# Mixture-of-experts stage: gathered tokens in batches of four chunks, half of the transposes in another PSUM bank, one bias sum

## The chip, the core and the metric

One core of a Trainium2 chip runs the kernel as one program. The time is device time in microseconds (us) of one execution. Runs of the kernel before lie at 1731.54, 1734.95 and 1739.19 us, median 1734.95 us. The profile is one execution of its own.

## The reference, cut to what matters

The program is two transformer layers over 256 tokens of width 1024. Only the last part matters here: 32 experts, each token goes to 4 of them. The experts' weights are 32 x (1024 x 2048 + 1024 x 1024) float32 numbers.

```python
logits = xt @ w_router + b_router
top_val, top_idx = lax.top_k(logits, TOP_K)          # 4 of 32
gates = softmax(top_val)
# for each expert e, with the rows xb of its tokens:
hb = clamped_swiglu(xb @ w_gu[e] + b_gu[e])          # 1024 -> 2 x 1024
yb = hb @ w_down[e] + b_down[e]                      # 1024 -> 1024
y[tok] += gate * yb
```

## The kernel before, in words

Everything up to the router takes the first 740 us and is not touched. Then comes the loop over experts (`for e in range(NE - 2)`, L1635), which is what the change edits. Each expert gets 64 token places (`CAP`).

**Weights.** A weight tile is 128 partitions x 16 KB, 2 MB in all. An expert has four such tiles of `w_gu` and two of `w_down`. They land in a ring of twelve slots (`slot_tile`, L1469): the tile of number n may be loaded when the last reader of tile n - 12 is through. All loads are issued by SyncE's queue (SP) in one order, that of the program: the four tiles of gate and up of expert e+1, then the two of down of expert e. The bias matrix `b_down` takes a slot of this ring too: `load_b_down` (L1401) is called in iteration 15, after the tiles of that iteration, and its slot goes on to the twelfth tile behind it, which is the second down tile of expert 17.

**One iteration e.** `make(0)` and `make(1)` (L1524) turn the two halves of the gate and up result of expert e with four TensorE transposes each into a PSUM bank, from where VectorE and ScalarE make the activation `u_`. `front(e + 1)` runs the gate and up product of the next expert (L1511, 64 instructions, 8 in each of 8 steps k). Inside it, after given k, stand `make(1)`, the `scatter` of expert e-1 (L1566, adds the expert's output to the four accumulator banks) and `slots_of(e)` (L1444 and L1445, tokens to places). Last comes `dn_product` (L1556, 32 instructions), whose bank is read by ScalarE into `yh` (L213) and by VectorE into `yl` (L214).

**Gathering tokens.** Every second iteration (e even) `group` makes the inputs of the next two experts. `chunk(c)` (L1456) is four TensorE instructions for 128 of the 1024 features, 128 columns wide, into a bank with the tag `tr`, and one evacuation into `xg` by VectorE (L1462). Eight chunks stand between the steps of `dn_product`. `xg` has one buffer, so that its first chunk can be written only when the product that reads the old one has ended.

**PSUM.** Eight banks: four accumulators, two with the tag `mm` for the gate and up product, one `tr`, one `y`. `tr` serves the transposes of `make(0)` and `make(1)`, `turn_slots`, the chunks and the transposes of the gates; `y` serves the down product.

**Bias of the down product.** `add_b_down(odd)` (L1405) runs after the down products of iterations 15 and 16, each time with its own copy and transposes of the gates and with four products (eight instructions) over half of the columns. It is the last reader of the bias slot.

**Order.** The program's order is a first draft. The framework plans the order of each engine's instructions from its own table of costs, keeps the order within a queue fixed from then on, and sets the semaphores; the trace shows the order that came out. Each engine works its queue in order. After the loop follow a branch for experts with more than 64 tokens (L1606), the last two experts and the final norm.

Of the kernel before, what the change touches and what calls it, by code (L numbers as in the profile page):

```python
# [11 lines left out]
F32 = mybir.dt.float32  # L12
# [5 lines left out]
ALU = mybir.AluOpType  # L18
# [4 lines left out]
P = 128  # L23
T = 256
# [3 lines left out]
NE = 32  # L28
# [15 lines left out]
def kernel(ctx: ExitStack, tc: tile.TileContext, A, out, probe=None, stop=None):  # L44
# [46 lines left out]
    def ps(name, tag="mm"):  # L91
        return pst["pool"].tile([P, 512], F32, tag=tag, name=name, bufs=pst["tags"][tag])
# [177 lines left out]
    def half(h):  # L270
        return slice(h * 512, (h + 1) * 512)
# [1120 lines left out]
        V.tensor_copy(cnt_i[:, NE:NE + 1], cmax)  # L1392

    yh, yl, sT = (mp.tile([P, w], F32R, name=t) for t, w in (("yh", 512), ("yl", 512), ("sT", T)))
    u_ = mp.tile([P, 2, 4, CAP], F32, name="u_")
    bd = {}

    def load_b_down():  # L1400
        bd["t"] = slot_tile()  # L1401
        for q in range(4):
            ld(bd["t"][q * NE:(q + 1) * NE, :256], A["b_down_2"][0, :, q * 256:(q + 1) * 256])

    def add_b_down(odd):  # L1405

        g4 = small.tile([P, 2, 4, NE], F32, tag="SX", name="g4", bufs=1)
        V.tensor_copy(g4, gate.unsqueeze(2).to_broadcast([P, 2, 4, NE]))
        bd4, gT = bd["t"][:, :256], bd["t"][:, 256:512]
        pt = ps("gT_ps", "tr")  # L1410
        for b in range(2):
            PE.transpose(pt[:, b * P:(b + 1) * P], g4[:, b].rearrange("p q e -> p (q e)"), ident)
        V.tensor_copy(gT, pt[:, :T])
        for b in range(2):
            for h in range(2):
                q = 2 * h + odd
                rows_ = slice(q * NE, (q + 1) * NE)
                PE.matmul(acc[b][h][:, odd * 256:(odd + 1) * 256], gT[rows_, b * P:(b + 1) * P], bd4[rows_, :],
                          start=False, stop=False, tile_position=(q * NE, 0))

    def one_hot(pos_cols, n, name):

# [7 lines left out]
    def norm_hot(pos_cols, n, name):  # L1430

        s_ = small.tile([P, 2, n, CAP], F32, tag="SX", name=f"SX{name}", bufs=1)
        for b in range(2):
            for o in range(n):
                last["V"] = V.tensor_scalar(s_[:, b, o, :], iota_s, pos_cols[:, b, o:o + 1], rm[:, b:b + 1],
                                            op0=ALU.is_equal, op1=ALU.mult)
        return s_
# [13 lines left out]
    def gather(s_, n, name, xg=None):  # L1451

        if xg is None:
            xg = small.tile([P, 8, n * CAP], F32, tag="xg", name=f"xg{name}", bufs=1)

        def chunk(c, on_v=False, tag="tr"):  # L1456
            po = ps(f"xg{name}_{c}", tag)
            for b in range(2):
                PE.matmul(po[:, :n * CAP], x_t[:, b, every(2, c)], s_[:, b].rearrange("p o s -> p (o s)"),  # L1459
                          start=b == 0, stop=b == 1)  # L1460
            if on_v:
                V.tensor_scalar(xg[:, c, :], po[:, :n * CAP], ffn_g(c), None, op0=ALU.mult)  # L1462
            else:
                S.activation(xg[:, c, :], po[:, :n * CAP], AF.Copy, scale=ffn_g(c))
        return xg, chunk

    slot = [len(gu0)]

# [52 lines left out]

    def swiglu(gs, bcol, name, u_=u_):

        def make(h):  # L1524
            pt = ps(f"gt{name}_{h}", "tr")
            for c in range(4):

                PE.transpose(pt[:, c * P:(c + 1) * P], gs[:, every(4, 4 * h + c)], ident)  # L1528
            pv = pt.rearrange("p (c q s) -> p c q s", c=4, q=2)

            g_, t_ = (gs[:, 512 * h + 256 * i:512 * h + 256 * (i + 1)].rearrange("p (c s) -> p c s", c=4)
                      for i in range(2))
            u = u_[:, h]
            V.tensor_tensor(g_, pv[:, :, 0, :],  # L1534
                            bcol[:, 4 * h:4 * h + 4].unsqueeze(2).to_broadcast([P, 4, CAP]), op=ALU.add)
            V.tensor_tensor(u, pv[:, :, 1, :],  # L1536
                            bcol[:, 8 + 4 * h:12 + 4 * h].unsqueeze(2).to_broadcast([P, 4, CAP]), op=ALU.add)
            V.tensor_scalar(g_, g_, 7.0, None, op0=ALU.min)  # L1538
            V.tensor_scalar(u, u, 7.0, -7.0, op0=ALU.min, op1=ALU.max)
            S.activation(t_, g_, AF.Tanh, scale=0.851)  # L1540
            V.scalar_tensor_tensor(u, u, 1.0, g_, op0=ALU.add, op1=ALU.mult)
            V.scalar_tensor_tensor(u, t_, 1.0, u, op0=ALU.add, op1=ALU.mult)
        return make

    def dn_product(wt, gslot, name, chunk=None, u_=u_, tag="y", between=None):

        po = ps(f"dn{name}", tag)
        for k in range(8):
            if chunk:
                chunk(k, True)  # L1550
            for f in (between or {}).get(k, ()):
                f()
            if k % 4 == 0:
                w = wt(k // 4)
            for cg in range(2):
                PE.matmul(po[cg * CAP:(cg + 1) * CAP, :], u_[:, k // 4, k % 4, :],  # L1556
                          w[:, k % 4, cg * 512:(cg + 1) * 512], start=k == 0, stop=k == 7)
        hilo(yh, yl, po, scale=gslot() if callable(gslot) else gslot)
# [17 lines left out]

    def group(g):
        pos_cols = pos1[:, :, g * GR:(g + 1) * GR]
        st["xg"], chunk = gather(norm_hot(pos_cols, GR, f"g{g}"), GR, f"g{g}")
        return chunk  # L1580

    def front(e, between):
        if e == EOVER + 1:
# [7 lines left out]
    def slots_of(e):  # L1591
        st["gslot", e] = turn_slots(one_hot(pos1[:, :, e:e + 1], 1, f"e{e}")[:, :, 0], gate3[:, :, e, :], f"e{e}")

    chunk = group(0)
    first = {k: [lambda k=k: chunk(k + 1, k % 2 == 0, ("tr", "y")[(k + 1) % 2])] for k in range(1, 7)}
    first[0] = [lambda: chunk(0), lambda: chunk(1, True, "y")]
    first[1].append(lambda: seed(1))
# [4 lines left out]
    def overflow():  # L1602
        wsl = [slot_tile() for _ in range(2)]
        oxg = st["keep"][:, D:D + D // 2].rearrange("p (c s) -> p c s", c=8)
        most = nc.values_load(cnt_i[0:1, NE:NE + 1], min_val=0, max_val=T)
        with tc.If(most > CAP):  # L1606
            with tc.For_i(0, NE, 1) as e:
                ne = nc.values_load(cnt_i[0:1, bass.ds(e, 1)], min_val=0, max_val=T)
                with tc.If(ne > CAP):
                    pc = small.tile([P, 2, 1], F32, tag="pc", name="pc", bufs=1)  # L1610
                    gc = small.tile([P, 2, 3], BF16, tag="gc", name="gc", bufs=1)
                    bc = small.tile([P, 16], F32, tag="bc", name="bc", bufs=1)
                    V.tensor_copy(pc, pos1[:, :, bass.ds(e, 1)])
                    V.tensor_copy(gc, gate3[:, :, bass.ds(e, 1), :].rearrange("p b o q -> p b (o q)"))
                    V.tensor_copy(bc, bgu[:, :, bass.ds(e, 1)].rearrange("p c o -> p (c o)"))

                    def by_turns(src, n):
                        return lambda m: piece(src, m, wsl[m % 2], n)

                    for blk in range(1, T // CAP):  # L1620
                        V.tensor_scalar(pc, pc, float(CAP), None, op0=ALU.subtract)
                        _, chunk = gather(norm_hot(pc, 1, f"o{blk}"), 1, f"o{blk}", oxg)
                        s_ = one_hot(pc, 1, f"o{blk}")
                        gslot = turn_slots(s_[:, :, 0], gc, f"o{blk}")
                        wg = w_gu[bass.ds(e, 1)].rearrange("o k c -> (o k) c")
                        wd = w_dn2[bass.ds(e, 1)].rearrange("o k c -> (o k) c")
                        g0 = gu_out(gu_product(by_turns(wg, 2), oxg, 0, f"o{blk}",
                                               {k: [lambda k=k: chunk(k)] for k in range(8)}), f"o{blk}")
                        make = swiglu(g0, bc, f"o{blk}")
                        make(0)  # L1630
                        make(1)
                        dn_product(by_turns(wd, 4), gslot, f"o{blk}")
                        scatter()

    for e in range(NE - 2):  # L1635
        make = swiglu(gs, bgu[:, :, e], f"e{e}")
        make(0)
        between = {1: [lambda: make(1)], 4: [lambda: slots_of(e)]}
        if e and e - 1 != EOVER:
            between[3] = [scatter]  # L1640
        gs = front(e + 1, between)
        wd = load_dn(w_dn2[e])
        if e == 15:
            load_b_down()
        if e == EOVER:

            wg1 = load_gu(w_gu[e1])
            wd0, wd1 = load_dn(w_dn2[e0]), load_dn(w_dn2[e1], parts=True)
        if e == 2:
            counts()  # L1650
        chunk = group(e // GR + 1) if e % GR == 0 else None
        dn_product(wd, st["gslot", e], f"e{e}", chunk)
        if e in (15, 16):
            add_b_down(e - 15)

    scatter()
    overflow()
# [69 lines left out]
```

## Time and profile before

| | |
|---|---|
| runs | 1731.54, 1734.95, 1739.19 us (median 1734.95) |
| the profiled execution's own time | 1733.49 us |
| its span, first to last instruction | 1731.8 us |
| TensorE matmul (PE) busy | 1634.4 us, 94% |
| VectorE (DVE) busy | 744.4 us, 43% |
| ScalarE (ACT) busy | 511.2 us, 30% |
| granted TensorE clock, mean | 0.991 |
| DMA moved | 527.57 MB, mean 305 GB/s |

The share of busy time is a mean over very different stages. For the expert loop one looks at two of its iterations at a time (an even and an odd one, since only even ones gather), at what TensorE waits for in them, and at the rate at which the weights arrive. A row of a timeline gives the start and the length in us, engine, line, operation, output and inputs, the shape, how many instructions are merged in it, and in brackets how long the engine sat idle before it and which operation ended that.

### The profile page before, as it was taken

Reading aid. Unit: us, or ns where it says so; the run is one execution under the profiler, and the core shown is the slowest. Engines: PE = TensorE matmul, PEld = TensorE weight load, DVE = VectorE, ACT = ScalarE, POOL = GpSimd, SP = SyncE. Lnnn points to the kernel's source line nnn. Section 1 sums busy time; section 2 is a strip of 40 time slices with the busy share of each in tenths; the row PEclk is TensorE's granted clock in tenths of the full one; section 3 lists DMA queues with packets and bytes.
Section 4 is the critical chain, followed back from the end, with each engine's and each line's share of the span. In section 5 each row is a group of like instructions: output and inputs, shape, how many; then the busy total and the mean of one; then the engine's idle time right before and its main releaser. Section 6 shows DMA issues by size and latency. Waiting matters only on the chain. (4 is left out here: it accounts for less than half of the span.)

```text
span 1731.8 us, 23231 instructions
## 1 busy us (share of the span) xinstructions
PE 1634.4 (94%) x9279; PEld 1014.7 (59%) x9280; DVE 744.4 (43%) x1705; ACT 511.2 (30%) x959; POOL 221.5 (13%) x319
## 2 busy tenths in 40 slices
PE   8899999999999999999999999999999999999987
PEld 8887799989999788863333333333333333333332
DVE  5867755567777776533232222212222321222113
ACT  4465554555555565521110110001101100110011
POOL 6988412200010000000000000000000000000000
PEclk9999999999999999999999999999999999999999
DMA  9852355654646535489999999999949999999992
GB/s 287 255 166 67 104 183 184 217 192 161 214 147 207 162 126 192 171 354 427 428 425 428 428 427 428 428 427 427 399 177 426 428 427 427 426 428 428 426 425 106
DMA packets 139413, 527.57 MB, mean 305 GB/s; under 512 B 11105, under 2 KB 99206, under 8 KB 114694
## 3 DMA queue, kind: packets, MB, share of 16 engines
q1 hardware_dynamic: 139302, 526.05, 77.3%
q8 instruction: 74, 1.21, 0.3%
q14 instruction: 37, 0.30, 0.1%
HBM read 524.95 MB, written 4.22 MB: 306 GB/s over the span
## 5 line engine op out<-in xcount | busy, mean ns | idle before, releaser
L1511 PE MATMUL gue<-raw,xgg 128*64 128x512 f32 x2032 | 455.6, 596 | 0.0
L189 DVE TENSOR_TENSOR wl<-raw,wh 128x1024 fp32r<-128x1024 f32 (+3 forms) x218 | 273.8, 1257 | 179.0 <-ACT wh L188 178.5
L188 ACT CAST wh<-raw 128x1024 fp32r<-128x1024 f32 (+2 forms) x220 | 227.8, 1035 | 257.7 <-PE g L197 64.7
L1511 PEld LDWEIGHTS gue<-raw,xgg 128*64 128x64 f32 x2032 | 138.6, 137 | 254.9 <-issue 242.4
L1556 PE MATMUL dne<-raw,u__8494 128*64 128x512 f32 x992 | 234.0, 607 | 0.0
L1462 DVE TENSOR_SCALAR xgg<-xgg,v_c 128x128 f32<-128x128 f32 x124 | 43.5, 351 | 387.9 <-PE gue L1511 195.5
L1519 ACT COPY gse<-gue 128x512 f32<-128x512 f32 x62 | 36.3, 586 | 345.7 <-PE gue L1511 345.7
L1556 PEld LDWEIGHTS dne<-raw,u__8494 128*64 128x64 f32 x992 | 65.4, 138 | 109.9 <-issue 100.9
L1459 PEld LDWEIGHTS xgg<-SXg,x_t 128*128 128x128 f32 x512 | 70.1, 196 | 99.1 <-DVE xgg L1462 57.6
L1459 PE MATMUL xgg<-SXg,x_t 128*128 128x128 f32 x512 | 94.2, 307 | 34.0 <-DVE xgg L1462 33.0
L1687 POOL TENSOR_TENSOR ssl<-ssl,nhalf 128x1 f32<-128x1 f32 x2 | 1.1, 558 | 969.2 <-DVE ssl L1686 969.2
L1534 DVE TENSOR_TENSOR gse<-gte,bgu 128x256 f32<-128x256 f32 x62 | 26.3, 425 | 194.6 <-PE gte L1528 185.8
L213 ACT ACTIVATE yh<-dne,gslote 128x512 fp32r<-128x512 f32 x32 | 22.0, 688 | 253.5 <-PE dne L1556 253.5
L388 POOL TENSOR_TENSOR convo<-convo,prod 128x256 f32<-128x256 f32 x90 | 76.9, 854 | 7.4
L1540 ACT ACTIVATE gse<-gse 128x256 f32<-128x256 f32 x62 | 25.8, 417 | 165.5 <-DVE gse L1538 165.5
L196 PE MATMUL g<-h_h,wh 128*128 128x256 f32 x256 | 73.1, 286 | 0.0
L197 PE MATMUL g<-h_l,wh 128*128 128x256 f32 x256 | 73.1, 285 | 0.0
L198 PE MATMUL g<-h_h,wl 128*128 128x256 f32 x256 | 72.9, 285 | 0.0
L1528 PEld LDWEIGHTS gte<-ident,gse 128*128 128x128 f32 x248 | 35.7, 209 | 62.5 <-issue 49.5
L387 POOL TENSOR_SCALAR prod<-hconv,v_c 128x256 f32<-128x256 f32 x90 | 68.0, 756 | 8.6
L1536 DVE TENSOR_TENSOR u__8494<-gte,bgu 128x256 f32<-128x256 f32 x62 | 26.0, 419 | 74.7 <-PE dne L1556 74.7
L1528 PE MATMUL gte<-ident,gse 128*128 128x128 f32 x248 | 49.7, 314 | 8.7 <-DVE u__8494 L1536 8.7
(804 smaller groups left out, 3047.3 us busy)
## 6 DMA issues: line engine op xcount, KB each, us to landing
raw<-in_w_gu_dram SPq DMA_DIRECT2D x127, 2048.0 KB
raw<-in_w_down_dram SPq DMA_DIRECT2D x63, 2048.0 KB
raw<-in_w_in_dram SPq DMA_DIRECT2D x32, 1024.0 KB
raw<-in_w_up_dram SPq DMA_DIRECT2D x22, 1024.0 KB
raw<-in_w_down_dram SPq DMA_DIRECT2D x12, 1024.0 KB
raw<-in_w_out_dram SPq DMA_DIRECT2D x8, 1024.0 KB
raw<-in_w_ckv_dram SPq DMA_DIRECT2D x8, 1024.0 KB
raw<-in_w_in_dram SPq DMA_DIRECT2D x13, 512.0 KB
```

The lines of the kernel that those rows point to most:

```text
L188: S.copy(hi, src)
L189: last["lo"] = (eng or V).tensor_sub(lo, src, hi.bitcast(F32))
L196: PE.matmul(o, wh[:, k, :], ah[:, k, :], start=first and k == 0, stop=False)
L197: PE.matmul(o, wh[:, k, :], al[:, k, :], start=False, stop=False)
L198: PE.matmul(o, wl[:, k, :], ah[:, k, :], start=False, stop=last and k == nk - 1)
L387: G.tensor_scalar(prod[0][:, :T], hconv[:, c, k:k + T], w, 0.0, op0=ALU.mult, op1=ALU.add)
L388: G.tensor_add(convo[:, c, :], convo[:, c, :], prod[0][:, :T])
L1459: PE.matmul(po[:, :n * CAP], x_t[:, b, every(2, c)], s_[:, b].rearrange("p o s -> p (o s)"), start=b == 0, stop=b == 1)
L1462: V.tensor_scalar(xg[:, c, :], po[:, :n * CAP], ffn_g(c), None, op0=ALU.mult)
L1511: PE.matmul(pgu[n][cg * CAP:(cg + 1) * CAP, :], xg[:, k, col:col + CAP], w[:, k % 2, cg * D + n * 512:cg * D + (n + 1) * 512], start=k == ...
L1528: PE.transpose(pt[:, c * P:(c + 1) * P], gs[:, every(4, 4 * h + c)], ident)
L1556: PE.matmul(po[cg * CAP:(cg + 1) * CAP, :], u_[:, k // 4, k % 4, :], w[:, k % 4, cg * 512:(cg + 1) * 512], start=k == 0, stop=k == 7)
```

## The change

Three edits, all in the expert loop.

1. `gather` gets a third function, `four(h)`: it puts four chunks side by side into one `tr` bank (4 x 128 columns) and evacuates them with one VectorE operation, which multiplies with the gains spread over the columns. `four(0)` stands ahead of step 0 of the down product, `four(1)` ahead of step 4, in place of eight chunks. The first group keeps its chunks.
2. `make(1)` writes its transposes to the bank `y` in place of `tr`, in all iterations of the loop.
3. The bias sum is done once, in iteration 15: `b_down` is loaded as two halves of 512 columns (two DMAs in place of four), `gates_down` turns the gates ahead of step 4 of the down product, `add_b_down` adds four products of 512 columns ahead of step 6.

```diff
     def load_b_down():
         bd["t"] = slot_tile()
-        for q in range(4):
-            ld(bd["t"][q * NE:(q + 1) * NE, :256], A["b_down_2"][0, :, q * 256:(q + 1) * 256])
+        for h in range(2):
+            ld(bd["t"][h * NE:(h + 1) * NE, :512], A["b_down_2"][0, :, half(h)])
...
+    def gates_down():
+        g2 = small.tile([P, 2, 2, NE], F32, tag="SX", name="g2", bufs=1)
+        V.tensor_copy(g2, gate.unsqueeze(2).to_broadcast([P, 2, 2, NE]))
         pt = ps("gT_ps", "tr")
         for b in range(2):
-            PE.transpose(pt[:, b * P:(b + 1) * P], g4[:, b].rearrange("p q e -> p (q e)"), ident)
-        V.tensor_copy(gT, pt[:, :T])
+            PE.transpose(pt[:2 * NE, b * P:(b + 1) * P], g2[:, b].rearrange("p q e -> p (q e)"), ident)
+        V.tensor_copy(bd["t"][:2 * NE, 512:512 + T], pt[:2 * NE, :T])
+    def add_b_down():
         for b in range(2):
             for h in range(2):
-                q = 2 * h + odd
-                rows_ = slice(q * NE, (q + 1) * NE)
-                PE.matmul(acc[b][h][:, odd * 256:(odd + 1) * 256], gT[rows_, b * P:(b + 1) * P], bd4[rows_, :],
-                          start=False, stop=False, tile_position=(q * NE, 0))
+                rows_ = slice(h * NE, (h + 1) * NE)
+                PE.matmul(acc[b][h], bd["t"][rows_, 512 + b * P:512 + (b + 1) * P], bd["t"][rows_, :512],
+                          start=False, stop=False, tile_position=(h * NE, 0))
...
+        def four(h, tag="tr"):
+            po = ps(f"xg{name}_h{h}", tag)
+            w = n * CAP
+            for i in range(4):
+                for b in range(2):
+                    PE.matmul(po[:, i * w:(i + 1) * w], x_t[:, b, every(2, 4 * h + i)],
+                              s_[:, b].rearrange("p o s -> p (o s)"), start=b == 0, stop=b == 1)
+            gains = vec["ffn"].rearrange("p (j k) -> p k j", j=2)[:, 2 * h:2 * h + 2, :]
+            V.tensor_tensor(xg[:, 4 * h:4 * h + 4, :].rearrange("p (k j) s -> p k j s", j=2),
+                            po[:, :4 * w].rearrange("p (k j s) -> p k j s", k=2, j=2),
+                            gains.unsqueeze(3).to_broadcast([P, 2, 2, w]), op=ALU.mult)
...
-        between = {1: [lambda: make(1)], 4: [lambda: slots_of(e)]}
+        between = {1: [lambda: make(1, "y")], 4: [lambda: slots_of(e)]}
...
-        chunk = group(e // GR + 1) if e % GR == 0 else None
-        dn_product(wd, st["gslot", e], f"e{e}", chunk)
-        if e in (15, 16):
-            add_b_down(e - 15)
+        between = {}
+        if e % GR == 0:
+            _, four = group(e // GR + 1)
+            between = {0: [lambda: four(0)], 4: [lambda: four(1)]}
+        if e == 15:
+            between = {4: [gates_down], 6: [add_b_down]}
+        dn_product(wd, st["gslot", e], f"e{e}", between=between)
```

## Rows read from the trace of the kernel before

**Rows 1.** The page, span in 40 slices of 43.3 us: what the DMA moved.
```profile
GB/s 287 255 166 67 104 183 184 217 192 161 214 147 207 162 126 192 171 354 427 428 425 428 428 427 428 428 427 427 399 177 426 428 427 427 426 428 428 426 425 106
```
**Rows 2.** Windows of two iterations: length, busy us and counts, PEclk, DMA share, GB/s.
```profile
904.54:963.47 58.93, 54.99 (x266) 21.32 (x265) 14.43 (x46) 6.13 (x12) 0.00 (x0) 1.00 1.00 426
...
1022.41:1082.98 60.57, 56.63 (x266) 21.69 (x264) 14.43 (x46) 6.13 (x12) 0.00 (x0) 0.97 1.01 428
...
1202.51:1263.68 61.17, 57.01 (x277) 22.41 (x276) 16.15 (x50) 6.13 (x12) 0.00 (x0) 1.00 1.00 409
1263.68:1324.05 60.37, 55.82 (x276) 22.01 (x272) 14.05 (x45) 6.13 (x12) 0.00 (x0) 1.00 0.59 246
1324.05:1382.99 58.94, 55.01 (x267) 21.32 (x266) 14.44 (x46) 6.13 (x12) 0.00 (x0) 1.00 1.01 427
```
**Rows 3.** Timeline of PE over one such pair, 904 to 966 us.
```profile
909.57 0.74 PE L1459 MATMUL xgg<-SXg,x_t 128*128 128x128 f32 x4
910.23 10.52 PE L1511 MATMUL gue<-raw,xgg 128*64 128x512 f32 x48
921.21 0.74 PE L1459 MATMUL xgg<-SXg,x_t 128*128 128x128 f32 x4 [0.45 <-DVE xgg L1462]
922.39 0.74 PE L1459 MATMUL xgg<-SXg,x_t 128*128 128x128 f32 x4 [0.44 <-DVE xgg L1462]
...
924.24 3.65 PE L1556 MATMUL dne<-raw,u__8494 128*64 128x512 f32 x16
...
937.25 0.50 PE L1566 MATMUL acc<-yl,sT 64*128 64x512 f32 x2 [0.41 <-DVE yl L214]
...
958.38 0.72 PE L1528 MATMUL gte<-ident,gse 128*128 128x128 f32 x4 [0.62 <-DVE u__8494 L1536]
959.03 3.65 PE L1556 MATMUL dne<-raw,u__8494 128*64 128x512 f32 x16
963.21 0.22 PE L1444 MATMUL ste<-ident_b,Se 128*128 128x128 bf16 x1 [0.53 <-DVE u__8494 L1536]
...
963.47 0.73 PE L1566 MATMUL acc<-yh,sT 64*128 64x512 f32 x4
```
**Rows 4.** Waits of PE, 844.5 to 1681 us: us in total, times, longest.
```profile
PE xgg L1459 <- DVE xgg L1462: 31.2, 70, 0.5
PE gte L1528 <- DVE u__8494 L1536: 8.0, 13, 0.6
PE ste L1444 <- DVE u__8494 L1536: 6.8, 13, 0.5
```
**Rows 5.** DMA queue: bytes landed from 692 to 805 us, and from 1296 to 1670.9 us.
```profile
q1 hardware_dynamic: 2915, 33.89, 73.0%
...
q1 hardware_dynamic: 10910, 159.01, 100.0%
```
**Rows 6.** Timeline of SP, 1180 to 1360 us, around the bias tile.
```profile
1207.65 1.72 SPq L1403 DMA_DIRECT2D raw<-in_b_down_dram  x4
...
1261.81 34.99 SPq L1481 DMA_DIRECT2D raw<-in_w_down_dram  x2
1296.85 2.27 SPq L1481 DMA_DIRECT2D raw<-in_w_gu_dram  x4
```
**Rows 7.** Timeline of PE: second half of down product 17, whole of product 29.
```profile
1319.61 3.65 PE L1556 MATMUL dne<-raw,u__8494 128*64 128x512 f32 x16
...
1667.51 7.04 PE L1556 MATMUL dne<-raw,u__8494 128*64 128x512 f32 x32
```
**Rows 8.** Instructions by form, 800 to 1680 us: busy us, mean ns, idle before.
```profile
L1462 DVE TENSOR_SCALAR xgg<-xgg,v_c 128x128 f32<-128x128 f32 x120 | 42.1, 351 | 372.1 <-PE gue L1511 195.5 <-PE xgg L1459 176.5
...
L214 DVE SCALAR_TENSOR_TENSOR yl<-dne,gslote,yh 128x512 fp32r<-128x512 f32 x30 | 22.4, 746 | 17.5 <-ACT yh L213 17.5
...
L213 ACT ACTIVATE yh<-dne,gslote 128x512 fp32r<-128x512 f32 x30 | 20.6, 688 | 248.1 <-PE dne L1556 248.1
...
L1418 PE MATMUL acc<-raw 32*128 32x256 f32 x16 | 2.3, 400 | 0.5 <-DVE raw L1413 0.5
```

More of the change, by code (lines that the diff above doesn't have):

```diff
@@ L1401, in load_b_down @@
         bd["t"] = slot_tile()
-        for q in range(4):
-            ld(bd["t"][q * NE:(q + 1) * NE, :256], A["b_down_2"][0, :, q * 256:(q + 1) * 256])
[L1405 to L1409, printed above, removed]
+        for h in range(2):
[3 more added lines that the diff above has]
+        V.tensor_copy(g2, gate.unsqueeze(2).to_broadcast([P, 2, 2, NE]))
         pt = ps("gT_ps", "tr")
         for b in range(2):
-            PE.transpose(pt[:, b * P:(b + 1) * P], g4[:, b].rearrange("p q e -> p (q e)"), ident)
-        V.tensor_copy(gT, pt[:, :T])
+            PE.transpose(pt[:2 * NE, b * P:(b + 1) * P], g2[:, b].rearrange("p q e -> p (q e)"), ident)
+        V.tensor_copy(bd["t"][:2 * NE, 512:512 + T], pt[:2 * NE, :T])
+    def add_b_down():
         for b in range(2):
             for h in range(2):
-                q = 2 * h + odd
-                rows_ = slice(q * NE, (q + 1) * NE)
-                PE.matmul(acc[b][h][:, odd * 256:(odd + 1) * 256], gT[rows_, b * P:(b + 1) * P], bd4[rows_, :],
-                          start=False, stop=False, tile_position=(q * NE, 0))
+                rows_ = slice(h * NE, (h + 1) * NE)
+                PE.matmul(acc[b][h], bd["t"][rows_, 512 + b * P:512 + (b + 1) * P], bd["t"][rows_, :512],
+                          start=False, stop=False, tile_position=(h * NE, 0))
     def one_hot(pos_cols, n, name):
@@ L1464, in chunk @@
                 S.activation(xg[:, c, :], po[:, :n * CAP], AF.Copy, scale=ffn_g(c))
-        return xg, chunk
+        def four(h, tag="tr"):
[9 more added lines that the diff above has]
+                            gains.unsqueeze(3).to_broadcast([P, 2, 2, w]), op=ALU.mult)
+        return xg, chunk, four
     slot = [len(gu0)]
@@ L1522, in swiglu, with make @@
     def swiglu(gs, bcol, name, u_=u_):
-        def make(h):
-            pt = ps(f"gt{name}_{h}", "tr")
+        def make(h, tag="tr"):
+            pt = ps(f"gt{name}_{h}", tag)
             for c in range(4):
@@ L1543, in swiglu, with dn_product @@
         return make
-    def dn_product(wt, gslot, name, chunk=None, u_=u_, tag="y", between=None):
+    def dn_product(wt, gslot, name, u_=u_, tag="y", between=None):
         po = ps(f"dn{name}", tag)
         for k in range(8):
-            if chunk:
-                chunk(k, True)
             for f in (between or {}).get(k, ()):
@@ L1578, in group @@
         pos_cols = pos1[:, :, g * GR:(g + 1) * GR]
-        st["xg"], chunk = gather(norm_hot(pos_cols, GR, f"g{g}"), GR, f"g{g}")
-        return chunk
+        st["xg"], *how = gather(norm_hot(pos_cols, GR, f"g{g}"), GR, f"g{g}")
+        return how
     def front(e, between):
@@ L1592, in slots_of @@
         st["gslot", e] = turn_slots(one_hot(pos1[:, :, e:e + 1], 1, f"e{e}")[:, :, 0], gate3[:, :, e, :], f"e{e}")
-    chunk = group(0)
+    chunk, _ = group(0)
     first = {k: [lambda k=k: chunk(k + 1, k % 2 == 0, ("tr", "y")[(k + 1) % 2])] for k in range(1, 7)}
@@ L1621, in overflow @@
                         V.tensor_scalar(pc, pc, float(CAP), None, op0=ALU.subtract)
-                        _, chunk = gather(norm_hot(pc, 1, f"o{blk}"), 1, f"o{blk}", oxg)
+                        _, chunk, _ = gather(norm_hot(pc, 1, f"o{blk}"), 1, f"o{blk}", oxg)
                         s_ = one_hot(pc, 1, f"o{blk}")
```

## The prediction, made before the changed kernel was run

> **What bounds the kernel now.** I read the page's slices first, then windows, PE's timeline, the waits and the two DMA views. The slices [rows 1] show the expert loop as a flat stretch of 425 to 428 GB/s from slice 18 on, with one hole (399, 177) near 1255 to 1299 us. At such a rate one suspects the DMA. The windows [rows 2] show that two resources run level. A pair of iterations lasts 58.93 to 58.94 us in eight of twelve windows, to a hundredth, with a DMA share of 1.00 to 1.01; twelve tiles of 2.097 MB at 427 GB/s also take 58.9 us (4.91 a tile). Which one sets the pace is told by the hole: in the window at 1263.68 the DMA is busy for 0.59 of the time and the pair is still 60.37 us long. And none of PE's nine kinds of wait in 844.5 to 1681 us ends on a DMA: those on VectorE come first [rows 4]. So PE is the bound, its instructions and its waits for VectorE, and the weights are ahead of it.
>
> How far ahead matters, because a faster PE eats that lead. From 692 to 805 us 33.89 MB landed, 16.2 tiles [rows 5]; when down product 0 starts, near 805 us, it needs the eighth of them, so the lead is at most 8 tiles, 39 us. The hole costs (427 - 409) x 61.17 + (427 - 246) x 60.37 = 12.03 MB, 28.2 us of DMA time [rows 2]. Its cause is in SP's queue [rows 6]: the bias tile is issued at 1207.65, and the two down tiles issued from 1261.81 take 34.99 us, since the second (expert 17) needs the bias tile's slot, which the second `add_b_down` frees only behind product 16. That load leaves near 1296.8 and is used at 1319.61 [rows 7], so PE never waited. At the end, 159.01 MB landed between 1296 and 1670.9 us [rows 5], 75.8 tiles. Counted from that load, the second down tile of expert 29 is the 73rd (six an expert), and its use starts in the middle of the 7.04 us row at 1667.51 [rows 7]: a lead of 2.8 tiles, 13.9 us.
>
> **The change part by part.** The sum is made against the profiled execution (1733.49 us); the median of the runs, 1734.95, is 1.46 above it and I add that at the end.
>
> *Gather.* Today five chunks of eight wait for the evacuation of the one before: 0.44 or 0.45 us idle, and from start to start 922.39 - 921.21 = 1.18 us where an unhindered chunk takes 910.23 - 909.57 = 0.66 [rows 3]. That is 0.52 a chunk, 2.6 us a group. The columns that PE streams stay the same. The new evacuation is 512 columns out of PSUM; the nearest rows are 0.746 us for 512 columns (L214) and 0.351 for 128 (L1462) [rows 8], so VectorE spends 1.5 us a group in place of 2.8, hidden as now. New is the wait of `four(1)` for `four(0)`'s evacuation. At the low end it is 0: as written, 16 instructions of the down product lie between (3.65 us at 924.24 [rows 3]). At the high end `four(1)` stands directly behind, waits 0.746 and the 0.17 that a stalled chunk pays beyond its 0.351, together 0.92. I take 0.92, since today's order has the early chunks at 921.21 and 922.39, ahead of the down product, not between its steps as the program has them. Behind a waiting `four(1)` stand the down product and everything after it on PE. Net gain 1.7 us a group.
>
> *Transposes on another bank.* In odd iterations the second transposes wait 0.62 us (958.38) until VectorE has read the first half out of `tr` [rows 3]. VectorE is late there because it must first see the down product finish with `u_`. With `y` they don't share a bank with the first half, and that wait goes. The bank `y` itself is held by the running down product, so these transposes can't stay inside it; they move behind it, into the next gate and up product. There a new wait is possible, for the evacuations into `yh` and `yl`. Low end 0: in the program a step of eight instructions stands ahead (48 take 10.52 us [rows 3], so 1.75), more than ScalarE's 0.688 and VectorE's 0.746 together [rows 8]. High end: first in the queue behind the product, 0.688 + 0.746 + 0.17 = 1.6 us in every iteration, 3.2 a pair. I take 0; the nearest row is the scatter at 937.25, which needs the same `yl` and waits 0.41 [rows 3], and that wait is there today. The 0.53 before the places' matmuls (963.21) goes as well, but the scatter behind them starts at 963.47 when `yh` is just ready, so that wait only changes its name: 0, high end 0.53. Gain 0.62 a pair.
>
> *Bias sum.* The two windows with it are 2.24 and 1.44 us longer than 58.93 [rows 2], 3.7 in all. What stays is the columns: sixteen products, 2.3 us [rows 8], now eight of twice the width. One copy and turning of the gates falls away. I take a gain of 1.4, between 0 and 2.3. The larger part is off PE: the slot comes free some 30 us sooner, while the load that needs it stands eleven tiles (54 us) behind the bias tile, so the hole closes. By itself this is worth 0, because PE did not wait there; it is the cover for the other two edits. Two DMAs in place of four on SP's queue are within its 1.72 us row [rows 6], and nothing waits for them.
>
> *Sum.* A pair gains 1.7 + 0.62 = 2.3 us. Fifteen groups and as many odd iterations lie ahead of the last regular down product: 34.8, with the bias 36.2 us. The ends of a pair are 2.6 + 0.62 + 0.53 = 3.75 us (57.6 with the bias) and 2.3 - 3.2 = -0.9 (a loss of 12).
>
> *What is late next.* The weights. The last regular down product may start earlier by no more than its lead and the closed hole, 13.9 + 28.2 = 42 us, less some part of a tile's 4.91 us, since PE can begin on a tile only when all of it has landed: I take 2, between 0 and 4.9. So beyond 40 us every gain on PE turns into waits for DMA. With 2.3 a pair the lead falls from 39 to about 4 us and is just not used up. After that product the branch, the last two experts and the norm are as before, all on PE's path.
>
> The Trainium skill, "DMA: Bandwidth & Descriptors", section "Where 436 GB/s comes from", holds that loads from HBM are limited to about 358 GB/s a core, and to 435 by the fabric. By 358 a pair would need 70 us of DMA and no edit on PE could bring anything; by 435 it would need 57.8 and the limit of 40 us would be some 17 us further off. The trace decides for neither: 427 GB/s at a share of 1.01 [rows 2], which is what that page measured for 16 MB (425).
>
> **The rivals.**
>
> 1. *A slower kernel: waits change their place.* With single banks and queues in order, the price depends on what the planned order puts directly behind a bank's reader. Should it put `four(1)` behind `four(0)` (0.92), `make(0)` behind `four(1)` (0.92) and `make(1)` behind each down product (2 x 1.6), a pair has 5.0 us of new waits against 3.75 that go: 1.3 slower, fifteen times, less 1.4: 18 us, 1753 us. It decides from 3.75 us of new waits a pair. For it: today's odd iterations do use the place inside the down product that `y` forbids. Against: eight instructions of other work stand ahead in the program.
> 2. *The hole stays.* If the last reader of the bias tile is planned behind the next product, the limit is 13.9 - 2 = 12 us: 1723 us. For it: the order is planned, not written. Against: today's first bias sum directly follows product 15, and the slot is wanted eleven tiles later.
> 3. *Half of the gain.* Some new waits of the second kind, one of 0.8 us a pair: (2.3 - 0.8) x 15 + 1.4 = 24 us, 1711 us.
> 4. *The clock falls when PE begins to wait for tiles.* Today it falls seldom; a window with one fall shows 0.97 and 60.57 us against 58.94 [rows 2], 1.63 us. One more fall in each of 15 pairs takes 24.5 of the 36 us: 1723 us. Against: pairs with 3.9 us of idle PE (58.93 - 54.99) keep 1.00 [rows 2], and my sum has PE waiting for almost no tile. The Trainium skill, "TensorE: Matmul & The Clock Gate", section "HAM oscillation — how this bites in real kernels", describes such a loop, in which each wait for a DMA halves the clock for the work behind it; no run here shows it yet.
> 5. *Nothing changes*, because the order comes out with other waits of the same sum: 1735 us.
>
> **How the numbers follow.** The forecast is 1733.49 - 36.2 = 1697.3 on the profiled execution, 1699 us on the median. Its own range is 1693 to 1707: the limit of the DMA with nothing lost on a tile at the lower end, a wait of 0.5 us a pair at the upper. Chances: forecast 0.66, rival 3 0.14, rival 2 0.06, rival 4 0.03, rival 5 0.03, rival 1 0.08. The range runs from 1687 (a DMA stream a little quicker than the limit worked out) to 1722 and leaves out rivals 1, 2, 4 and 5, 0.20. About 0.5%, 8.7 us, is what a measurement of this kernel can tell from no change: faster by more has 0.66 + 0.14 + 0.06 + 0.03, less 0.01 for the near edge, 0.88; within it 0.04; slower 0.08.
>
> **What would show it.** Right: windows of a pair at 56 to 57 us while the lead lasts, then at most 58.9; DMA share 1.0 in the windows of iterations 14 to 17 as well, and no SP row of 35 us behind the bias tile; in PE's waits the 31.2 us for the gather's evacuation fall to under 14, and the transposes' 8.0 vanish; the first waits of PE for `raw` tiles, if any, near the end. `four(1)` ahead of the down product with some 0.75 us idle shows the 0.92, between its steps with none shows 2.6 a group and a stop at the limit of 40. Wrong: pairs at 58.9 us with PE waiting for DMA from the middle on at an unclosed hole (rival 2); new waits of `gte` on `yl` above 1 us (rivals 1 and 3); a granted clock under 0.95 in the windows (rival 4).

## The result, and the profile after

The changed kernel takes 1717.22 us (median of 4 runs, 1716.20 to 1718.83), the kernel before, beside it on the same chip, 1734.26 (4 runs, 1731.54 to 1739.19): ratio 0.9899, 95% interval 0.9875 to 0.9924. It is faster by 17 us where 36 were forecast. The profiled execution took 1718.83 us, with a span of 1717.1.

What the DMA moved, as in [rows 1] (slices of 42.9 us): the hole is closed.

```profile
GB/s 288 258 162 66 106 184 184 209 183 177 200 178 161 188 123 184 185 307 428 427 427 427 428 427 427 428 428 426 417 427 428 427 426 428 428 427 427 427 336 74
```

Windows of a pair, as in [rows 2]: length, PE, PEld, DVE, ACT and POOL busy, granted clock, DMA share, GB/s. The last two have the bias sum.

```profile
1076.14:1134.54 58.40, 53.81 (x264) 21.25 (x264) 13.03 (x39) 6.12 (x12) 0.00 (x0) 1.00 1.01 428
1192.94:1254.47 61.53, 56.29 (x274) 21.98 (x274) 13.59 (x41) 6.12 (x12) 0.00 (x0) 1.00 1.01 420
1254.47:1312.13 57.66, 53.79 (x264) 21.15 (x264) 13.04 (x39) 6.12 (x12) 0.00 (x0) 1.00 1.01 428
```

A pair gains 0.53 us, not 2.3. PE works 1.2 us less (53.81 against 54.99) and waits 0.65 us more (4.59 against 3.94). The timeline of PE over one pair, as in [rows 3], shows where:

```profile
1083.00 2.15 PE L1472 MATMUL xgg_h<-SXg,x_t 128*128 128x128 f32 x16 [0.66 <-DVE gslote L1448]
1085.09 10.52 PE L1524 MATMUL gue<-raw,xgg 128*64 128x512 f32 x48
1096.40 2.15 PE L1472 MATMUL xgg_h<-SXg,x_t 128*128 128x128 f32 x16 [0.79 <-DVE xgg L1475]
1098.48 3.65 PE L1567 MATMUL dne<-raw,u__8494 128*64 128x512 f32 x16
1102.07 0.75 PE L1541 MATMUL gte<-ident,gse 128*128 128x128 f32 x4
1103.73 0.23 PE L1444 MATMUL ste<-ident_b,Se 128*128 128x128 bf16 x1 [0.92 <-DVE u__8494 L1549]
...
1103.98 3.65 PE L1567 MATMUL dne<-raw,u__8494 128*64 128x512 f32 x16
1108.42 0.73 PE L1577 MATMUL acc<-yh,sT 64*128 64x512 f32 x4 [0.79 <-ACT yh L213]
1109.21 0.75 PE L1541 MATMUL gte<-ident,gse 128*128 128x128 f32 x4
...
1129.87 0.22 PE L1444 MATMUL ste<-ident_b,Se 128*128 128x128 bf16 x1 [0.53 <-DVE u__8494 L1549]
...
1130.10 3.65 PE L1567 MATMUL dne<-raw,u__8494 128*64 128x512 f32 x16
1134.54 0.73 PE L1577 MATMUL acc<-yh,sT 64*128 64x512 f32 x4 [0.79 <-ACT yh L213]
```

Four chunks run from 1083.00 to 1085.09, 0.52 us each (0.66 before). `four(1)` waits 0.79 us for `four(0)` as foreseen. The transposes `gte` wait no more: they stand behind the scatter's first four instructions. But the order of the others changed. `turn_slots` (`ste`) now stands in the middle of each down product, directly behind `make(0)` on the bank `tr`, and waits there for VectorE to read `make(0)`'s result, 0.92 and 0.53 us. In [rows 3] its four instructions lay between the down product and the scatter in the odd iteration (963.21), and the scatter at 963.47 found `yh` ready. With nothing in that place the scatter's wait for ScalarE, 0.79 us, is bare in both iterations. The waits of PE from 844.5 to 1655 us, as in [rows 4], say the same in sums:

```profile
PE acc L1577 <- ACT yh L213: 21.3, 27, 0.8
PE ste L1444 <- DVE u__8494 L1549: 19.7, 27, 0.9
PE xgg_h L1472 <- DVE xgg L1475: 11.1, 14, 0.8
PE xgg_h L1472 <- DVE gslote L1448: 7.9, 12, 0.7
```

31.2 us for the gather became 11.1, and 8.0 for the transposes and 5.2 for the scatter's `yl` are gone. In their place stand 21.3 for `yh`, 19.7 in place of 6.8 for `ste`, and 7.9 in place of 0.7 before `four(0)`: it writes to `tr`, and so waits until VectorE has read the result of `turn_slots` there (L1448). All kinds together make 61.8 us where the same iterations of the kernel before have 53.5.

The granted clock is a part of the 17 us. In the thirteen runs of the kernel before that the first experiments brought (on another chip), the time follows the mean clock: at 0.993 it takes 1730.0 and 1730.5 us, at 0.987 it takes 1737.9 to 1739.0. The changed kernel at 0.993 takes 1718.0 and 1718.8. At the same clock the change brings some 12 us. The rest of the 17 goes with a clock that fell less often (0.993 to 0.995 in its four runs, mostly 0.987 to 0.991 before); why it fell less is open.

### The profile page after: what moved, and what is told of

The parts are those of the page before. It is cut to its first block, busy times and chain, and to the rows that moved or that the text cites. A ratio compares the mean times of both kernels' runs of the same rounds, so it can differ in the third digit from the quotient of the medians.

```text
span 1717.1 us, 23092 instructions
## 1 busy us (share of the span) xinstructions
PE 1613.4 (94%) x9269; PEld 1013.2 (59%) x9270; DVE 721.5 (42%) x1613; ACT 510.9 (30%) x959; POOL 221.1 (13%) x319
## 5 line engine op out<-in xcount | busy, mean ns | idle before, releaser
L1567 PE MATMUL dne<-raw,u__8494 128*64 128x512 f32 x992 | 227.5, 598 | 0.0
L1475 DVE TENSOR_TENSOR xgg<-xgg_h,v_c 128x512 f32<-128x512 f32 x30 | 20.7, 691 | 222.4 <-PE gue L1524 177.4
L1472 PE MATMUL xgg_h<-SXg,x_t 128*128 128x128 f32 x480 | 64.8, 288 | 19.4 <-DVE xgg L1475 11.1
L1472 PEld LDWEIGHTS xgg_h<-SXg,x_t 128*128 128x128 f32 x480 | 58.9, 196 | 38.9 <-DVE xgg L1475 23.4
L214 DVE SCALAR_TENSOR_TENSOR yl<-dne,gslote,yh 128x512 fp32r<-128x512 f32 x32 | 24.0, 750 | 113.7 <-ACT yh L213 113.7
L196 PE MATMUL ffg<-h_h,wh 128*128 128x256 f32 x176 | 50.4, 287 | 0.0
```

Of the source, the lines that this page charges most:

```text
L196: PE.matmul(o, wh[:, k, :], ah[:, k, :], start=first and k == 0, stop=False)
L1472: PE.matmul(po[:, i * w:(i + 1) * w], x_t[:, b, every(2, 4 * h + i)], s_[:, b].rearrange("p o s -> p (o s)"), start=b == 0, stop=b == 1)
```

## The experiments

Ratios are against the kernel before on the same chip. Its medians in the three rounds of experiments and beside the changed kernel are 1733.26 to 1734.75 us, so that times of different rounds can be compared to some 1.5 us.

**gather_alone, y_alone, bias_alone, no_y.** Each edit alone, and the change without edit 2. Theory A: edit 2 costs what edit 1 gains, by the order it brings. Rival B: edit 1 itself is worth little.

```diff
 no_y (against the changed kernel):
-        between = {1: [lambda: make(1, "y")], 4: [lambda: slots_of(e)]}
+        between = {1: [lambda: make(1)], 4: [lambda: slots_of(e)]}
 gather_alone: this, and load_b_down and add_b_down of the kernel before
 y_alone (against the kernel before):
-        between = {1: [lambda: make(1)], 4: [lambda: slots_of(e)]}
+        between = {1: [lambda: make(1, "y")], 4: [lambda: slots_of(e)]}
 bias_alone: load_b_down, gates_down and add_b_down of the change, eight chunks, tr
```

> Only edit 1 (four chunks in one tr bank); transposes on tr and two bias sums as before. Theory A (the transposes on bank y cost more than they save, by moving turn_slots into the down product and baring the scatter's wait for yh): waits of PE in a pair of iterations 3.4 us (0.79 for four(1), 0.9 and 0.6 for the second transposes, 0.53 twice for the places), eight chunks 1.1 us denser, pair 57.3 us against 58.94 before and 58.40 after; time about 1710 us, faster than the changed kernel. Rival B (the gather's own new waits eat the gain, the y bank is neutral or helps): pair 58.4 to 59.0, time 1718 to 1733.

Measured 1705.53 us (1704.83 to 1706.30), ratio 0.9829 (0.9806 to 0.9852).

> Only edit 2 (second transposes on bank y). Theory A: the wait of 0.62 us before the second transposes goes, but the places' matmuls move into the odd down product and the scatter's wait for yh (0.79) is bare: pair 58.7 to 59.3 us, time within 4 us of before. Rival B (neutral or a gain of its own): pair 58.3 or less, 10 us or more faster than before.

Measured 1754.13 us (1753.16 to 1755.48), ratio 1.0109 (1.0085 to 1.0133).

> Only edit 3 (one bias sum in iteration 15). Both theories: the hole in the DMA stream closes, DMA share 1.0 in every pair, and the time falls by no more than 1.4 to 2.5 us, since PE never waited for the weights; pair 58.94 as before. If the hole did cost time after all: 10 us or more faster.

Measured 1737.10 us (10 runs, 1729.57 to 1738.84), ratio 1.0001 (0.9984 to 1.0018).

> The changed kernel with edit 2 taken back (second transposes on tr again). Theory A: pair 57.3 us in place of 58.40, time about 1707 us, 10 us or more faster than the changed kernel (1717). Rival B: pair 58.4 or more, not faster than the changed kernel.

Measured 1703.64 us (1703.05 to 1704.95), ratio 0.9821 (0.9798 to 0.9845).

So edit 1 alone brings 29 us, more than the whole change. Edit 2 costs 19 us alone and 13.6 us inside the change. Edit 3 alone is worth nothing that can be measured. Not all expectations were met. gather_alone and no_y are 3 to 5 us faster than theory A said, at 1 us less a pair. y_alone was to stay within 4 us of the kernel before and missed that by far. In bias_alone the hole is gone, but the DMA does not run at full rate everywhere: some slices of its page from there on show 400 to 417 GB/s. A pair in gather_alone, no_y and y_alone, one window each:

```profile
1012.67:1068.99 56.32, 52.74 (x266) 21.06 (x264) 12.99 (x40) 6.13 (x12) 0.00 (x0) 1.00 1.01 427
```
```profile
1040.17:1096.49 56.32, 52.74 (x266) 21.06 (x265) 12.99 (x40) 6.13 (x12) 0.00 (x0) 1.00 1.01 427
```
```profile
967.45:1027.65 60.20, 55.34 (x265) 21.62 (x265) 14.29 (x45) 6.13 (x12) 0.00 (x0) 1.00 1.01 427
```

Edit 1 takes 2.61 us off a pair, edit 2 alone adds 1.27. In y_alone (844.5 to 1700 us) the wait before `ste` is as in the kernel before, 6.8 us; what has grown is the scatter's for `yh` (0.8 before) and the chunks' until the result of `turn_slots` is read (0.7 before):

```profile
PE acc L1566 <- ACT yh L213: 11.0, 14, 0.8
PE xgg L1459 <- DVE gslote L1448: 9.1, 13, 1.2
```

So alone edit 2 also loses by what its new order bares, but by another set of waits than inside the change. The waits of PE in gather_alone, 844.5 to 1640 us, show that the gather's gain is not the waits:

```profile
PE gte L1540 <- DVE u__8494 L1548: 21.5, 26, 1.4
PE ste L1443 <- DVE u__8494 L1548: 13.1, 25, 0.5
PE xgg_h L1471 <- DVE xgg L1474: 11.1, 14, 0.8
PE dne L1566 <- DMA raw<-in_w_down_dram: 3.1, 3, 1.3
PE gue L1523 <- DMA raw<-in_w_gu_dram: 2.8, 4, 1.2
```

31.2 us for the chunks fell to 11.1, but 8.0 for `gte` rose to 21.5 and 6.8 for `ste` to 13.1. A pair's idle time went from 3.94 only to 3.58 us. What fell is PE's busy time, 54.99 to 52.74. The groups by form, 844 to 1640 us here and 844 to 1675 us in the kernel before (14 gathers in each), tell of what (busy us, mean ns of one):

```profile
L1523 PE MATMUL gue<-raw,xgg 128*64 128x512 f32 x1792 | 395.1, 595 | 2.8 <-DMA raw<-in_w_gu_dram 2.8
L1566 PE MATMUL dne<-raw,u__8494 128*64 128x512 f32 x896 | 204.6, 598 | 3.1 <-DMA raw<-in_w_down_dram 3.1
L1471 PE MATMUL xgg_h<-SXg,x_t 128*128 128x128 f32 x448 | 60.5, 288 | 12.2 <-DVE xgg L1474 11.1 <-DVE gslote L1447 0.7 <-DVE cmax L1391 0.4
```
```profile
L1511 PE MATMUL gue<-raw,xgg 128*64 128x512 f32 x1792 | 400.2, 596 | 0.0
L1556 PE MATMUL dne<-raw,u__8494 128*64 128x512 f32 x898 | 211.2, 608 | 0.0
L1459 PE MATMUL xgg<-SXg,x_t 128*128 128x128 f32 x448 | 82.7, 307 | 32.2 <-DVE xgg L1462 31.2 <-DVE gslote L1448 0.7 <-DVE cmax L1391 0.4
```

The same 448 chunk instructions take 82.7 - 60.5 = 22.2 us less, 1.6 a gather, and the two products 11.7 us less (0.8): in these rows sixteen equal instructions in a row run denser than four groups of four among others, and the products are cut less often. No run changes the length of the rows alone.

**y_held.** What of edit 2 costs: the bank, or the place where `turn_slots` was planned? Here the transposes stay on `y`, and `turn_slots` is held behind the last instruction of the down product.

```diff
-                PE.matmul(po[cg * CAP:(cg + 1) * CAP, :], u_[:, k // 4, k % 4, :],
+                last["dn"] = PE.matmul(po[cg * CAP:(cg + 1) * CAP, :], u_[:, k // 4, k % 4, :],
...
+    def held(e):
+        with behind({"dn": last["dn"]} if e else {}):
+            slots_of(e)
...
-        between = {1: [lambda: make(1, "y")], 4: [lambda: slots_of(e)]}
+        between = {1: [lambda: make(1, "y")], 4: [lambda: held(e)]}
```

> The changed kernel, all three edits with the second transposes on bank y, and one thing added: turn_slots may not be planned ahead of the last instruction of the down product before it. Theory A (the bank itself costs little, the loss comes from the place to which the planner then moves turn_slots): its waits of 0.92 and 0.53 us go, it stands again under the wait for yh, pair 56.5 to 57.0 us in place of 58.40, time 1700 to 1706. Rival C (bank y itself costs it, by the transposes that must follow the down product): pair stays above 58, time 1713 or more.

Measured 1704.70 us (1703.96 to 1705.30), ratio 0.9829 (0.9805 to 0.9853), as without edit 2. One pair, the waits of PE from 844.5 to 1640 us, and the place on the timeline:

```profile
1041.36:1097.69 56.33, 53.51 (x264) 21.27 (x264) 13.37 (x39) 6.13 (x12) 0.00 (x0) 1.00 1.01 427
```
```profile
PE acc L1577 <- ACT yh L213: 15.4, 28, 0.8
PE xgg_h L1472 <- DVE gslote L1448: 7.9, 12, 0.7
```
```profile
1058.70 7.09 PE L1567 MATMUL dne<-raw,u__8494 128*64 128x512 f32 x32
1065.72 0.23 PE L1444 MATMUL ste<-ident_b,Se 128*128 128x128 bf16 x1
...
1066.57 0.73 PE L1577 MATMUL acc<-yh,sT 64*128 64x512 f32 x4 [0.54 <-ACT yh L213]
```

The wait of `ste` is gone (0.92 and 0.53 a pair), and its four instructions stand in the scatter's wait, of which 0.54 stays of 0.79: 1.45 + 0.50 = 1.95 of the 2.07 us between 58.40 and 56.33. So inside the change the place costs the time. The bank brings nothing on balance even so. In no_y, in the same window, the two waits that y_held no longer has are these:

```profile
PE gte L1541 <- DVE u__8494 L1549: 22.2, 27, 1.0
PE ste L1444 <- DVE u__8494 L1549: 14.2, 27, 0.5
```

Against them y_held has 15.4 for `yh` (0.8 in no_y), 7.9 before `four(0)` (0.7), and 0.77 us a pair more of PE's busy time (53.51 against 52.74), since a scatter's `yl` matmuls are cut in two there. Its pair is as long as that of no_y, 56.33 and 56.32.

**four_mm, both_mm.** Is PE still the bound at 1704? `four(1)` goes to a third bank (`mm`), which takes its wait away; in both_mm the second transposes use `mm` too and stand right behind the first.

```diff
 both, against no_y:
-            between = {0: [lambda: four(0)], 4: [lambda: four(1)]}
+            between = {0: [lambda: four(0)], 4: [lambda: four(1, "mm")]}
 both_mm only:
-        between = {1: [lambda: make(1)], 4: [lambda: slots_of(e)]}
+        make(1, "mm")
+        between = {4: [lambda: slots_of(e)]}
```

> The kernel without edit 2, and the second batch of four chunks goes to a bank of the gate and up product (tag mm) in place of tr. Its wait of 0.79 us and the 1.01 us of the transposes behind it should go: PE's own need is some 54.7 us a pair against 56.33. If the limit of the weight stream holds (40 us below before), the time stops at 1694 to 1697 and PE's waits for raw tiles grow from 6 us to 15 or more, pair 58.9 in the last iterations. If there is no such limit: 15 x 1.6 = 24 us below the kernel without edit 2, 1680.

Measured 1705.25 us (1703.62 to 1705.68), ratio 0.9834 (0.9811 to 0.9858).

> As the one before, and the second transposes go to a bank mm as well, called right behind the first. The 0.62 us before them go too; turn_slots moves into the down product, which may bare the wait for yh (0.79) as with bank y. PE's own need 54.5 to 55.5 us a pair. With the limit of the weight stream: same time as the one before within 2 us, 1693 to 1697. Without it: 1675 to 1685.

Measured 1704.03 us (1703.99 to 1705.13), ratio 0.9829 (0.9805 to 0.9852).

Both miss the 10 us more that my limit of 40 left. In both_mm an early and a late pair differ, and PE now waits for weights too (844.5 to 1640 us):

```profile
924.00:979.07 55.07, 52.34 (x264) 20.90 (x264) 13.36 (x40) 6.02 (x12) 0.00 (x0) 1.00 1.01 428
1432.77:1491.38 58.61, 52.87 (x266) 20.51 (x264) 13.18 (x39) 6.02 (x12) 0.00 (x0) 1.00 1.01 428
```
```profile
PE acc L1577 <- ACT yh L213: 22.1, 28, 0.8
PE gue L1524 <- DMA raw<-in_w_gu_dram: 16.8, 17, 1.7
PE dne L1567 <- DMA raw<-in_w_down_dram: 5.0, 8, 1.3
```

The first of these waits stands at 1322.76 us: there the lead is eaten, and from then on a pair lasts what its weights last. The last regular scatter starts at 1637.42 in no_y and 1675.33 in the kernel before: 37.9 us earlier. The last iterations of no_y wait for weights as well. So the limit of the loop is near the 40 that I gave; the rest was lost behind it, in a place that I had put down as unchanged. SP and PE at the end of no_y:

```profile
1628.02 10.06 SPq L1510 DMA_DIRECT2D raw<-in_w_down_dram  x3
1668.39 0.34 SPq L1494 DMA_DIRECT2D raw<-in_w_down_dram  x1
```
```profile
1670.04 0.75 PE L1541 MATMUL gte<-ident,gse 128*128 128x128 f32 x4
1675.98 5.63 PE L1567 MATMUL dne<-raw,u__8494 128*64 128x512 f32 x16 [5.19 <-DMA raw<-in_w_down_dram]
```

One tile, the second half of down product 30, is loaded apart from all others: its slot holds expert 30's gate and up result across the branch (`keep`). SP stood 27.0 us in the branch and issued this load at 1668.39, 1.4 us after the last byte of the others had landed (no DMA traffic from 1667 to 1669). In the kernel before it was issued at 1695.24, where the stream had ended near 1694, and used at 1708.56 without a wait. So this tile came only 26.9 us earlier and PE 37.9. PE stood 5.19 us for it and then ran the sixteen matmuls in 5.63 us in place of 3.65, at a mean granted clock of 0.63 over that stretch, so for a part of it at the lower level.

**no_y_late, y_held_late, both_late.** The slot of `keep` goes to the last half of expert 31's down weights, which are used some 10 us later; otherwise no_y, y_held and both_mm.

```diff
-            wd0, wd1 = load_dn(w_dn2[e0]), load_dn(w_dn2[e1], parts=True)
+            wd0, wd1 = last_downs()
...
+    def last_downs():
+        d0, d1 = [piece(w_dn2[e0], 0, slot_tile(), 4)], []
+        late = slot_tile().rearrange("p (j c) -> p j c", j=4)
+        d0.append(piece(w_dn2[e0], 1, slot_tile(), 4))
+        d1.append(piece(w_dn2[e1], 0, slot_tile(), 4))
...     (the three parts of expert 31's second tile into late)
```

> Without edit 2 (as no_y), and of the last four down-projection tiles the one that must take the slot of the kept gate/up result is now the last half of expert 31's weights, not the second half of expert 30's. Theory A (the faster versions all stop near 1704 because this one tile can only be fetched after the branch that ends the loop: issue at 1668.39, TensorE stands 5.19 us for it at 1675.98 and then takes 5.63 us at the half clock for 16 matmuls that take 3.65 otherwise): the wait and the 2.0 us behind it go, since expert 31 asks for its last half some 10 us later, and the median is 1703.6 - 5.2 - 2.0 = 1696 (1695 to 1698). Theory B (the weight stream as a whole ends no earlier than that; the wait only moves to another tile): within 2 us of 1703.6.

Measured 1697.97 us (1695.72 to 1699.45), ratio 0.9786 (0.9770 to 0.9803).

> The changed kernel with turn_slots held behind the down product (as y_held) and the same exchange of the last tiles. Theory A: the same 7 us, 1704.7 - 7.2 = 1697.5 (1696 to 1700). Theory B: within 2 us of 1704.7.

Measured 1696.28 us (1695.96 to 1699.16), ratio 0.9780 (0.9763 to 0.9796).

> The version with the shortest pair of iterations (as both_mm: 54.9 us until the weights hold it back, then 58.7) and the same exchange of the last tiles. Theory A: 1704.0 - 5.4 - 1.9 = 1696.7 (1695 to 1699), so no better than without the two extra banks: within the loop the weights' own rate, 58.7 us for a pair's 25.2 MB, is the limit. Theory B: within 2 us of 1704.0. If TensorE's shorter pair were worth something by itself, it would be more than 2 us below no_y_late.

Measured 1697.14 us (1695.89 to 1700.33), ratio 0.9790 (0.9774 to 0.9807).

All three gain 6 to 8 us on the versions without the exchange, as theory A said. The same two rows of no_y_late, without a wait:

```profile
1673.34 0.75 PE L1551 MATMUL gte<-ident,gse 128*128 128x128 f32 x4
1674.02 3.65 PE L1577 MATMUL dne<-raw,u__8494 128*64 128x512 f32 x16
```

The three are alike within their intervals, although both_late's pairs are shorter while the lead lasts. So about 37 us below the kernel before the weights decide. These are the best versions measured; y_held_late keeps all three edits. The exchange was not tried on the changed kernel itself, whose profile shows no wait at that tile.

## Why the prediction was wrong

*What bounds the kernel:* right. PE and its waits for VectorE set the pace, the weights were ahead, and they take over some 37 us further on.

*Transposes on another bank: the step that failed.* I wrote of the new waits "I take 0" and of the 0.53 us before the places' matmuls that it "only changes its name". Measured is a loss of 2.08 us a pair inside the change (58.40 against 56.32 in no_y) where I had a gain of 0.62. At the last scatter of the loop this makes 1660.77 - 1637.42 = 23.3 us; 7 us of it no_y gives back at the late tile. My high end (3.2 us of new waits a pair) was near in size and had the wrong place: I looked at the moved transposes, and these wait for nothing. What I did not price is the instructions that stay on the old bank. With `make(1)` out of `tr`, `turn_slots` is the next writer of `tr` behind `make(0)`, and the planned order puts it there at once. It waits for `make(0)`'s reader, and it no longer fills the scatter's wait for `yh`. y_held shows both. Against no_y a pair's rows give: `gte` 1.63 us less (0.62 and 1.01 there), `ste` 0.40 more, `yh` 1.58 more, `four(0)` 0.66 more, and PE's busy time 1.07 more (53.81 against 52.74), most of it from the scatter's `yl` matmuls, which the moved transposes cut into three and one. Half of the loss is thus no wait at all, and for that the prediction had no term.

*Gather:* right in sign, mis-sized, and for the wrong reason. I took 1.7 us a pair, between 1.7 and 2.6; measured alone is 2.61. `four(1)`'s wait is 0.79 where I had 0.92. But the 2.6 us of waits did not go: they came back before `gte` and `ste`, and idle PE fell by 0.36. The gain is 2.25 us of PE's busy time, which I took as fixed ("the columns that PE streams stay the same"). The columns do; the time that PE takes for them does not.

*Bias sum:* the two windows are 61.53 + 57.66 - 2 x 58.40 = 2.4 us longer than two others, 3.7 before: a gain of 1.3 for my 1.4. Alone it is within its uncertainty.

*The hole:* worth 0 by itself, right (bias_alone 1.0001). But the limit does not need edit 3. In gather_alone, without it, the hole's slice shows 420 GB/s, and the last regular scatter starts at 1640.94, 34.4 us earlier than before, where rival 2 had an unclosed hole and a limit of 12. My reading is that PE frees the slot, and a PE that is nearer to the stream frees it before the DMA runs dry: the hole shows how far the stream was ahead, and is not a loss beside that.

*The limit of 40 us:* near for the loop (37.9 in no_y), wrong for the end. "The branch, the last two experts and the norm are as before" holds for PE's work, not for the load that SP can issue only behind the branch. That took 7 us from each quicker version; with the exchange they reach 37 to 38 us below the kernel before.

*Rivals:* rival 1's mechanism was the right kind, another order that gives the waits back; of the three places that I named as its price only `four(1)` behind `four(0)` came (0.79), and that one my forecast had too. By result the case is rival 3's (1711, measured 1717): the gain was about halved, but by waits of `ste` and `acc` and by busy time, not by `gte` on `yl`. Rival 4 did not come. In both_mm PE waits 25 times for a tile in 844.5 to 1640 us, and the window from 1430 to 1637 us, with PE busy 183.42 of 207 us, shows a granted clock of 1.00:

```profile
1430.00:1637.00 207.00, 183.42 (x904) 69.60 (x900) 41.24 (x114) 20.30 (x40) 0.00 (x0) 1.00 1.01 427
```

The late tile's wait, 5.19 us in no_y, was followed by a stretch at the lower clock, and so was the branch's of 6.39 us in the changed kernel (0.50 from 1666 to 1672 us); these short ones, at most 1.7 us in both_mm and 2.7 in four_mm, were not. What set off the two falls in the loop of the kernel before is open. The section of the Trainium skill that I cited for this rival ("TensorE: Matmul & The Clock Gate", "HAM oscillation — how this bites in real kernels") describes a loop with waits for DMA of about 3 to 5 us. The late tile's wait, which is of that size, agrees with it; the loop's waits here are shorter than those that it describes.

The sum against the profiles: to its last scatter the changed kernel is 14.6 us earlier (1675.33 to 1660.77). 3.4 of it lie in iterations 0 and 1; twelve pairs at 0.53 make 6.4, the bias 1.3, and two falls of the clock that only the profile of before has 3.3; 0.2 is left.

## What to carry to other kernels

Giving one user of a shared PSUM bank another bank frees that user, and it changes who comes next on the old bank: list the writers in the new order, and price the wait of each, and what each had been covering. Here equal small matmuls in one row cost less of TensorE's time than the same ones in groups, so a batch can be worth more than the waits that it removes, and a move that cuts a row costs TensorE's time. A limit read from one resource's lead holds to the last place where that lead counts; behind it look for a load that cannot be issued early.

## What was not expected of the hardware

- Sixteen chunk matmuls in a row take 2.09 us from start to start, four take 0.66: 0.13 against 0.17 us each, with shape and operands unchanged.
- A scatter's four `yl` matmuls in one run take 1041.62 - 1040.95 = 0.67 us in no_y; cut into three and one, as in the changed kernel, they take 0.66 + 0.43 us by the same reading.
- The spread of the kernel before over its runs, 1730 to 1739 us, goes with the granted clock: 0.993 to 0.987.
- The weights' stream holds 427 GB/s at a DMA share of 1.01, also in the short pair of both_mm (55.07 us, 428 GB/s). Whether the transfers cost TensorE anything there was not tested.
- SP left the branch each time only when its loads had landed (stream's end and next issue: 1667 and 1668.39 in no_y, 1669 and 1669.97 in no_y_late, 1694 and 1695.24 before). In the changed kernel the stream ends near 1670 and the issue stands at 1678.80, but 8.2 us of that SP waits for VectorE to free the slot, behind the branch. That SP waits in the branch for its loads is read from these rows; it was not tested by itself.
